# Emitting the rounded copy of a weight piece at the end of the slot that frees its buffer, in the input projections

## The chip, the cores and the metric

The kernel runs on one core of a Trainium2 chip. The metric is the device time of one execution in microseconds (us). A core has five engines that are used here: TensorE (PE; its weight loads are shown apart as PEld), VectorE (DVE), ScalarE (ACT), GpSimd (POOL) and SyncE (SP), whose queue issues most of the DMAs. Each engine takes its instructions strictly in the order in which they were emitted, and waits on semaphores for the others.

## What is computed

One inference step of a two-layer backbone on 128 prompt tokens and 512 latent tokens of width 2048. Layer 0 has attention heads of two kinds (a windowed one with rotary embedding, and a neighbourhood one), layer 1 has bidirectional retention. Cut to the products that matter here:

```python
hp = rmsnorm(xp, norm_pre[l]) * (1.0 + sc_p[:, None]) + sh_p[:, None]
op, ka, va, kb, vb = even_context(hp, w_in_even[i], w_out_even[i], a_sink[i])
os_ = even_latent(hs, w_in_even[i], w_out_even[i], a_sink[i], na_rpb[i], ...)
op, sf, sb = retention_mixer(hp, w_in_odd[i], w_out_odd[i], ...)
xp = xp + g_p[:, None] * rmsnorm(op, norm_post[l])
```

So four large matrix products follow each other: `w_in_even`, `w_out_even`, `w_in_odd`, `w_out_odd`. Attention, retention and the modulation of layer 1 (`adaln`, a product of one vector with `w_ada`) are done beside them.

## The kernel before

**Slots.** The four projections are cut into 732 slots (`slots`, L268 to L278). A slot is one weight piece of 128 x 512 numbers and the matmuls that use it: 24 in a W slot with both token groups (L1370), 30 in an X slot (L1311). Of the 380 W slots of the two input projections, 156 belong to `w_in_even` and 224 to `w_in_odd`. Each product is made of three: the inputs stand in two parts, `hi` and `lo`, and so does each weight piece: `whi` is the piece rounded to fp32r by ScalarE (L291), `wlo` the rest, a subtraction on VectorE that reads `wraw` and `whi` (L292). Both are made in `split_slot`; `whi` and `wlo` have four buffers each, so the parts of slot s + 4 need the buffers that the matmuls of slot s release. The raw piece (`wraw`, five buffers) comes by DMA from SP's queue (`load_slot`, L282).

**What is emitted beside a slot.** At the head of each slot `step_all` takes one step of four lanes: `chain` (norms and residuals between the layers), `rope`, `heads` (attention, later retention) and `adal` (layer 1's modulation). A rope item of layer 0 multiplies on VectorE and GpSimd (L574, L575) and adds on VectorE (L578); one slot later the head's score matmul on TensorE reads the sum `qT` (L722). A block of a head is then a masked sum and maximum on VectorE (L688), an exponential on ScalarE (L698), a normalisation on VectorE (L705), a transpose on TensorE (L742), a copy on ScalarE (L744) and the product with the values (L753). An `adal` step multiplies one or two pieces `adaraw` into two sums `adaacc` on VectorE (L804); in 80 of its units the second product is made by ScalarE (`adaraw` in place, L801) and added by GpSimd (L802).

**Where the split stands.** `ahead(s)` makes the parts of slot s + 4 and issues the load of slot s + 7. `place(s)` says when. It is 2 for the W slots of both input projections: there `ahead(s)` is emitted in the next slot, behind that slot's `step_all`:

```python
step_all()
if s and place(s - 1) == 2:
    ahead(s - 1)
```

It is 1 for X slots and for `w_out_even` (`ahead(s)` at the end of slot s, behind the evacuation of PSUM), and 0 for `w_out_odd` (ahead of the evacuation).

Of the kernel before, what the change touches and what calls it, by code (L numbers as in the profile page):

```python
# [12 lines left out]
F32R = mybir.dt.float32r  # L13
BF16 = mybir.dt.bfloat16
AF = mybir.ActivationFunctionType
# [147 lines left out]
def body(tc, io):  # L163
    nc = tc.nc
# [24 lines left out]
    def dense():  # L189
        return psd.tile([128, 512], F32, name="ps_d", tag="d")  # L190
# [75 lines left out]
    whl = top.enter_context(tc.tile_pool(name="whl", bufs=4))  # L266
# [9 lines left out]
                    continue  # L276
                slots.append((job, kind, role, gs, u0 + u, half, 2 * u + half, 2 * n, w))
    NS = len(slots)  # L278
    raws, halves = {}, {}

    def load_slot(s):
        if s < NS:  # L282
            raws[s] = wraw.tile([128, 512], F32, name="wraw")
            nc.sync.dma_start(raws[s], io["wpack"][slots[s][4]][:, 512 * slots[s][5]:512 * slots[s][5] + 512])

    def split_slot(s):
        if s < NS:
            r = raws.pop(s)
            h = whl.tile([128, 512], F32R, name="whi")
            l = whl.tile([128, 512], F32R, name="wlo")  # L290
            nc.scalar.activation(h, r, AF.Copy)  # L291
            nc.vector.tensor_tensor(l, r, h.bitcast(F32), op=ALU.subtract)  # L292
            halves[s] = (h, l)

    first_ps = []
    with ExitStack() as st:
# [176 lines left out]
        while any(ln.busy() for ln in lanes0):  # L473
            for ln in lanes0:
                ln.step()
            loads(NU)
            if not order and main_loads < RAW:
                load_slot(main_loads)
                main_loads += 1
            while main_splits < main_loads - 1 and ("d", len(FIRST_SEQ) - 4 + main_splits) in done and not w_l.busy():  # L480
                split_slot(main_splits)
                main_splits += 1
# [3 lines left out]
    for i in range(4):  # L486
        if i >= main_splits:
            split_slot(i)
        if i < LEAD:
            load_slot(RAW + i)  # L490
# [11 lines left out]
    def step_all():  # L502
        for ln in lanes:
            ln.step()
# [365 lines left out]
    def norm_state(l):  # L870
        c = ctx.setdefault(("n", l), {})
        return c

    def evac_out(l, n, pss, gs):
        c = norm_state(l)
        cp = c["pool"]
        for gi in gs:
            a, b = GROUPS[gi]
            w = b - a
            ps = pss[gi]  # L880
            if ("acc", gi) not in c:
                c["acc", gi] = cp.tile([128, w], F32, name=f"acc{gi}")
                nc.scalar.activation(c["acc", gi], ps[:, :w], AF.Square)
            else:
                sq = cp.tile([128, 384], F32, name="sq", bufs=2)
                nc.scalar.activation(sq[:, :w], ps[:, :w], AF.Square)  # L886
                if n == KT - 1:
                    c["acc", gi] = [c["acc", gi], sq]
                else:
                    nc.gpsimd.tensor_tensor(c["acc", gi], c["acc", gi], sq[:, :w], op=ALU.add)  # L890
            for a2, b2, v in parts(a, b):
                nc.scalar.activation(y[:, n, a2:b2], ps[:, a2 - a:b2 - a], AF.Copy, scale=gg[l][:, n, v:v + 1])
            if n == 4 and gi == 0:
                for i in range((6, 8)[l]):
                    load_x(l, i)
            if n == KT - 1:
                queue_chain(l, gi)
# [132 lines left out]
    def open_layer1():  # L1030
        st = ExitStack()
        R["st"] = st
        R["qkv"] = st.enter_context(tc.tile_pool(name="qkv", bufs=1))
        R["norm"] = ExitStack()
        norm_state(0)["pool"] = R["norm"].enter_context(tc.tile_pool(name="nrm0", bufs=1))
# [250 lines left out]
    def y_split(k):  # L1286
        nc.scalar.activation(hi[:, k, :], y[:, k, :], AF.Copy)
        nc.vector.tensor_tensor(lo[:, k, :], y[:, k, :], hi[:, k, :].bitcast(F32), op=ALU.subtract)
# [11 lines left out]
    def drain(which):  # L1300
        while any(l.busy() for l in which):
            step_all()

    def X_matmuls(pss, h, l, k0, i, ni, gs):
        for kk in range(2):
            k = k0 + kk
            for p, (xp, wp) in enumerate(((hi, h), (hi, l), (lo, h))):
                for t in range(5):
                    c0 = TP + 128 * t if t < 4 else 0
                    j, o = (t // 2, 256 * (t % 2)) if t < 4 else (2, 0)  # L1310
                    mm(pss[j][:, o:o + 256], lhsT=xp[:, k, c0:c0 + 128], rhs=wp[:, 256 * kk:256 * kk + 256],  # L1311
                       start=(i == 0 and kk == 0 and p == 0 and t in (0, 2, 4)),
                       stop=(i == ni - 1 and kk == 1 and p == 2), skip_group_check=True)

    def ahead(s):

        split_slot(s + 4)
        load_slot(s + LEAD + RAW)

    def place(s):  # L1320

        w, kind = slots[s][8], slots[s][1]
        return PLACE[w, kind]
# [6 lines left out]
    s = 0  # L1330
    while s < NS:
        job, kind, role, gs, unit, half, i, ni, w = slots[s]
        if s == firsts["w_out_even"]:
            drain([rope, heads, adal])
            AB["st"].close()
            L0.close()
            open_layer1()
        if s == firsts["w_in_odd"]:
            pass
        if s == firsts["w_out_odd"]:  # L1340
            drain([heads])
            R["st"].close()
            norm1 = ExitStack()
            chain.new = 1
            norm_state(1)["pool"] = norm1.enter_context(tc.tile_pool(name="nrm1", bufs=1))
        i0 = KP // 4 if role[0] == "rest" else 0
        if i == i0:
            pss = {}
            if kind == "W":
                for gi in gs:  # L1350
                    pss[gi] = dense()
            else:
                for j in range(3):
                    pss[j] = dense()
# [3 lines that stand above are left out]
        if w == "w_in_odd" and i == 0:  # L1358
            chain.new = 2
            for gi in gs:  # L1360
                while ("h1", gi) not in done:
                    step_all()
        h, l = halves.pop(s)
        if kind == "W":
            for kk in range(4):
                k = 4 * i + kk
                for p, (wp, xp) in enumerate(((h, hi), (h, lo), (l, hi))):
                    for gi in gs:
                        a, b = GROUPS[gi]
                        mm(pss[gi][:, :b - a], lhsT=wp[:, 128 * kk:128 * kk + 128], rhs=xp[:, k, a:b],  # L1370
                           start=(k == 4 * i0 and p == 0), stop=(k == KT - 1 and p == 2))
        else:
            X_matmuls(pss, h, l, 2 * i, i, ni, gs)
        if place(s) == 0:
            ahead(s)
        if i == ni - 1:
            if w == "w_in_even":
                evac0(role, pss, gs)
            elif w == "w_in_odd":
                evac1(role, pss, gs)  # L1380
            else:
                evac_out(0 if w == "w_out_even" else 1, role[1], pss, gs)
        if place(s) == 1:
            ahead(s)
        if s in (end0, end1):
            drain([rope, heads] + ([adal] if s == end0 else []))
        for k in ysplit_at.get(s, ()):
            y_split(k)
        s += 1
# [123 lines left out]
```

## Time and profile before

| | |
|---|---|
| Median of 3 runs | 2534.35 us (2533.91 to 2534.43) |
| The profiled execution, its own time | 2534.7 us |
| Its span in the trace | 2532.9 us |
| Busy: PE, PEld, DVE, ACT, POOL | 97%, 94%, 59%, 40%, 15% of the span |
| `w_in_even` slots, by the matmul records of the trace | from 153 us to 989 us |
| `w_in_odd` slots, likewise | from 1231 us to 2278 us |

The span is 1.8 us shorter than the execution's own time, which is 0.35 us above the median. Engine times in the rows are counted from the span's start. A wait is put down to the instruction whose end released it.

### The profile page before, as it was taken

Reading aid. Unit: us, or ns where it says so; the run is one execution under the profiler, and the core shown is the slowest. Engines: PE = TensorE matmul, PEld = TensorE weight load, DVE = VectorE, ACT = ScalarE, POOL = GpSimd, SP = SyncE. Lnnn points to the kernel's source line nnn. Section 1 sums busy time; section 2 is a strip of 40 time slices with the busy share of each in tenths; the row PEclk is TensorE's granted clock in tenths of the full one; section 3 lists DMA queues with packets and bytes.
Section 4 is the critical chain, followed back from the end, with each engine's and each line's share of the span. In section 5 each row is a group of like instructions: output and inputs, shape, how many; then the busy total and the mean of one; then the engine's idle time right before and its main releaser. Section 6 shows DMA issues by size and latency. Waiting matters only on the chain.

```text
span 2532.9 us, 45640 instructions
## 1 busy us (share of the span) xinstructions
PE 2459.2 (97%) x17808; PEld 2383.1 (94%) x17808; DVE 1499.3 (59%) x2834; ACT 1006.8 (40%) x2140; POOL 389.6 (15%) x445
## 2 busy tenths in 40 slices
PE   5999999999999999999999999999999999999997
PEld 3699898999999999998999999999999999999996
DVE  6578787787777875338853535353525355363364
ACT  3233454443343335445653333233323333344443
POOL 1012221112112110114200101010101011011132
PEclk9999999999999999999999999999999999999998
DMA  9855444445545532436543121212121221215374
GB/s 373 319 171 178 148 138 145 127 136 183 174 155 172 174 132 86 160 131 224 188 159 128 63 80 63 88 59 86 61 88 59 80 80 63 80 59 179 124 238 130
DMA packets 186441, 347.12 MB, mean 137 GB/s; under 512 B 20912, under 2 KB 45872, under 8 KB 185712
## 3 DMA queue, kind: packets, MB, share of 16 engines
q1 hardware_dynamic: 182368, 333.25, 39.7%
q0 software_dynamic: 3712, 10.82, 1.2%
q8 instruction: 139, 2.28, 0.4%
q14 instruction: 78, 0.64, 0.1%
q10 hardware_dynamic: 144, 0.13, 0.0%
HBM read 325.51 MB, written 15.99 MB: 135 GB/s over the span
## 4 chain that ended last, share of the span: by engine, by line
PE 69%; DVE 4%; issue 2%; ACT 1%; DMA 1%; POOL 0%; SPq 0%; DVEq 0%; ACTq 0%; POOLq 0%
PE ps_d L1370 49%; PE ps_d L1311 12%; PE ps_O L1250 2%; DVE wlo L292 1%; DVE adaacc L804 1%; PE ps_O L1154 1%; PE ps_S L1154 1%; PE ps_O L753 1%; PE ps_T L1228 1%; ACT whi L291 1%; PE ps_S L1242 1%; DMA wraw<-i_wpack 0%; PE ps_T L742 0%; DVE y L974 0%; PE ps_T L1141 0%
## 5 line engine op out<-in xcount | busy, mean ns | idle before, releaser
L1370 PE MATMUL ps_d<-hi,whi 128*128 128x384 f32 (+1 forms) x3808 | 999.0, 316 | 0.7 <-ACT whi L291 0.6
L1370 PE MATMUL ps_d<-hi,wlo 128*128 128x384 f32 (+1 forms) x3808 | 977.1, 310 | 7.4 <-DVE wlo L292 7.0
L1370 PE MATMUL ps_d<-lo,whi 128*128 128x384 f32 (+1 forms) x3808 | 972.6, 309 | 0.0
L292 DVE TENSOR_TENSOR wlo<-wraw,whi 128x512 fp32r<-128x512 f32 x732 | 565.2, 775 | 595.8 <-ACT whi L291 591.0
L1370 PEld LDWEIGHTS ps_d<-hi,whi 128*128 128x128 f32 x3808 | 632.8, 189 | 11.7 <-issue 4.3
L1370 PEld LDWEIGHTS ps_d<-hi,wlo 128*128 128x128 f32 x3808 | 628.9, 189 | 13.0 <-DVE wlo L292 12.2
L1370 PEld LDWEIGHTS ps_d<-lo,whi 128*128 128x128 f32 x3808 | 628.2, 188 | 0.0
L291 ACT ACTIVATE whi<-wraw 128x512 fp32r<-128x512 f32 x732 | 454.8, 626 | 432.9 <-PE ps_d L1370 220.6
L804 DVE SCALAR_TENSOR_TENSOR adaacc<-adaraw,cvec,adaacc 128x512 f32<-128x512 f32 x400 | 276.8, 743 | 5.8 <-POOL adaacc L802 5.7
L802 POOL TENSOR_TENSOR adaacc<-adaacc,adaraw 128x512 f32<-128x512 f32 x80 | 103.0, 1288 | 714.0 <-ACT adaraw L801 711.2
L1311 PE MATMUL ps_d<-whi,hi 128*128 128x256 f32 x960 | 150.9, 287 | 0.8 <-ACT qT L654 0.8
L1311 PE MATMUL ps_d<-whi,lo 128*128 128x256 f32 x960 | 144.3, 280 | 0.0
L1311 PE MATMUL ps_d<-wlo,hi 128*128 128x256 f32 x960 | 144.3, 280 | 0.0
L801 ACT ACTIVATE adaraw<-adaraw,cvec 128x512 f32<-128x512 f32 x80 | 57.9, 724 | 207.7 <-DVE adaacc L804 149.3
L1311 PEld LDWEIGHTS ps_d<-whi,hi 128*128 128x128 f32 x960 | 128.0, 188 | 4.9 <-issue 1.4
L1311 PEld LDWEIGHTS ps_d<-wlo,hi 128*128 128x128 f32 x960 | 126.5, 188 | 0.0
L1311 PEld LDWEIGHTS ps_d<-whi,lo 128*128 128x128 f32 x960 | 126.5, 188 | 0.0
L890 POOL TENSOR_TENSOR acc<-acc,sq 128x384 f32<-128x384 f32 (+1 forms) x56 | 56.1, 1002 | 425.9 <-ACT sq L886 425.6
L698 ACT ACTIVATE p<-p,small 128x384 f32<-128x384 f32 (+1 forms) x64 | 42.9, 671 | 148.3 <-DVE small L690 148.3
L1146 DVE SCALAR_TENSOR_TENSOR fr<-ps_T,kdec,fr 128x256 fp32r<-128x256 f32 x64 | 31.0, 484 | 95.8 <-ACT fr L1145 95.8
L1235 ACT ACTIVATE sS<-sT 128x128 fp32r<-128x128 f32 x40 | 12.4, 311 | 147.9 <-DVE sT L1234 147.9
L1262 POOL TENSOR_TENSOR mv<-mv,mhalf 128x1 f32<-128x1 f32 x40 | 22.1, 552 | 299.5 <-DVE mv L1261 299.5
(248 smaller groups left out, 2427.8 us busy)
## 6 DMA issues: line engine op xcount, KB each, us to landing
wraw<-i_wpack SPq DMA_DIRECT2D x732, 256.0 KB, 2.8
adaraw<-i_ada SPq DMA_DIRECT2D x256, 256.0 KB, 2.7
sraw<-i_ada SPq DMA_DIRECT2D x64, 512.0 KB, 6.3
y<-i_xTp SPq DMA_DIRECT2D x4, 1280.0 KB, 8.6
wf<-i_wfirst SPq DMA_DIRECT2D x20, 256.0 KB, 5.9
bias<-i_biasB POOLq DMA_DIRECT2D x8, 640.0 KB, 4.9
x_scratch<-y SPq DMA_DIRECT2D x8, 384.0 KB, 3.8
xres<-x_scratch SPq DMA_DIRECT2D x8, 384.0 KB, 6.9
```

The lines of the kernel that those rows point to most:

```text
L291: nc.scalar.activation(h, r, AF.Copy)
L292: nc.vector.tensor_tensor(l, r, h.bitcast(F32), op=ALU.subtract)
L698: nc.scalar.activation(p[:, :nk], src, AF.Exp, bias=sm[:, 0:1], accum_out=sm[:, 1:2])
L801: nc.scalar.activation(r, r, AF.Copy, scale=cvec[:, kt, 1:2])
L802: nc.gpsimd.tensor_tensor(accs[1], accs[1], r, op=ALU.add)
L804: nc.vector.scalar_tensor_tensor(accs[v], r, cvec[:, kt, v:v + 1], accs[v], op0=ALU.mult, op1=ALU.add)
L890: nc.gpsimd.tensor_tensor(c["acc", gi], c["acc", gi], sq[:, :w], op=ALU.add)
L1146: nc.vector.scalar_tensor_tensor(t[:, 1, :], ps[:, :256], R["kdec"][:, d, h:h + 1], t[:, 0, :].bitcast(F32), op0=ALU.mult, op1=ALU.subtract)
L1154: mm(ps[:, 256 * d:256 * d + 256], lhsT=k[:, kp, 128 * d:128 * d + 128], rhs=v[:, vp, ch, :], start=(i == 0), stop=(i == 2))
L1250: mm(ab, lhsT=t["q"][:, qp, d, :], rhs=t["S"][d][sp].rearrange("p i e -> p (i e)"), start=(d == 0 and i == 0), stop=(d == 1 and i == 2))
L1311: mm(pss[j][:, o:o + 256], lhsT=xp[:, k, c0:c0 + 128], rhs=wp[:, 256 * kk:256 * kk + 256], start=(i == 0 and kk == 0 and p == 0 and t in ( ...
L1370: mm(pss[gi][:, :b - a], lhsT=wp[:, 128 * kk:128 * kk + 128], rhs=xp[:, k, a:b], start=(k == 4 * i0 and p == 0), stop=(k == KT - 1 and p = ...
```

## The change

In the W slots of the two input projections the rounded copy `whi` of slot s + 4 is emitted at the end of slot s, behind the evacuation. The subtraction `wlo` and the load stay where they were, behind the next slot's `step_all`. X slots and the output projections keep their order. Nothing is added or left out.

```diff
+    def split_hi(s):
+        if s < NS and s not in his:
+            h = his[s] = whl.tile([128, 512], F32R, name="whi")
+            nc.scalar.activation(h, raws[s], AF.Copy)
+
     def split_slot(s):
         if s < NS:
-            r = raws.pop(s)
-            h = whl.tile([128, 512], F32R, name="whi")
+            split_hi(s)
+            r, h = raws.pop(s), his.pop(s)
             l = whl.tile([128, 512], F32R, name="wlo")
-            nc.scalar.activation(h, r, AF.Copy)
             nc.vector.tensor_tensor(l, r, h.bitcast(F32), op=ALU.subtract)
             halves[s] = (h, l)
...
         if place(s) == 1:
             ahead(s)
+        elif place(s) == 2:
+            split_hi(s + 4)
```

The order of the instructions on VectorE, TensorE, GpSimd and SP is the same in both kernels; ScalarE's is not.

ScalarE in `w_in_even`, around the end of the fourth slot of one job, before (`wraw_2499` is the raw piece whose copy is followed here; `qT` and `rp` are the evacuation of a query head, `adaraw` the in-place product of the modulation):

```order
L291 ACTIVATE whi_2572<-wraw_2446 128x512
L609 ACTIVATE qT_2603<-ps_d_2416 128x128
L563 ACTIVATE rp_2602<-ps_d_2416 128x2x8x16
L564 ACTIVATE rp_2602<-ps_d_2417 128x2x8x16
L801 ACTIVATE adaraw_2565<-adaraw_2565,cvec_75 128x512
L291 ACTIVATE whi_2619<-wraw_2499 128x512
L291 ACTIVATE whi_2659<-wraw_2537 128x512
L801 ACTIVATE adaraw_2653<-adaraw_2653,cvec_75 128x512
L291 ACTIVATE whi_2696<-wraw_2576 128x512
```

The same place in the changed kernel:

```order
L805 ACTIVATE adaraw_2528<-adaraw_2528,cvec_75 128x512
L613 ACTIVATE qT_2603<-ps_d_2418 128x128
L567 ACTIVATE rp_2602<-ps_d_2418 128x2x8x16
L568 ACTIVATE rp_2602<-ps_d_2419 128x2x8x16
L289 ACTIVATE whi_2608<-wraw_2499 128x512
L805 ACTIVATE adaraw_2567<-adaraw_2567,cvec_75 128x512
L289 ACTIVATE whi_2649<-wraw_2537 128x512
L289 ACTIVATE whi_2689<-wraw_2576 128x512
L805 ACTIVATE adaraw_2655<-adaraw_2655,cvec_75 128x512
```

The copies of `wraw_2499` and `wraw_2576` stand ahead of the `adaraw` product that stood ahead of them.

ScalarE in `w_in_odd`, where a slot's steps transpose a retention key (`fr` is its rounded, decayed copy), before:

```order
L1072 ACTIVATE k1_15804<-ps_d_15638 128x256
L1145 ACTIVATE fr_15812<-ps_T_15809,kdec_15652 128x256
L291 ACTIVATE whi_15815<-wraw_15708 128x512
L1145 ACTIVATE fr_15866<-ps_T_15863,kdec_15652 128x256
L1145 ACTIVATE fr_15869<-ps_T_15863,kdec_15652 128x256
L291 ACTIVATE whi_15872<-wraw_15747 128x512
```

And in the changed kernel:

```order
L1076 ACTIVATE k1_15804<-ps_d_15638 128x256
L289 ACTIVATE whi_15807<-wraw_15708 128x512
L1149 ACTIVATE fr_15814<-ps_T_15811,kdec_15652 128x256
L289 ACTIVATE whi_15845<-wraw_15747 128x512
L1149 ACTIVATE fr_15868<-ps_T_15865,kdec_15652 128x256
L1149 ACTIVATE fr_15871<-ps_T_15865,kdec_15652 128x256
```

Each copy of a piece now stands ahead of the key copies of the next slot's head step.

## Rows read from the trace of the kernel before

**Rows 1.** Page: each engine's busy us (share of the span) xinstructions.

```profile
PE 2459.2 (97%) x17808; PEld 2383.1 (94%) x17808; DVE 1499.3 (59%) x2834; ACT 1006.8 (40%) x2140; POOL 389.6 (15%) x445
```

**Rows 2.** Busy us (xinstructions) of PE, PEld, DVE, ACT, POOL; clock; DMA share; GB/s.

```profile
153.00:515.00 362.00, 347.99 (x2485) 338.43 (x2484) 291.37 (x553) 158.64 (x346) 83.02 (x89) 0.99 0.48 152
515.00:975.00 460.00, 455.87 (x3484) 442.74 (x3483) 345.51 (x682) 180.52 (x386) 78.90 (x85) 1.00 0.48 156
...
1400.00:2200.00 800.00, 800.00 (x5842) 792.49 (x5841) 361.62 (x714) 261.01 (x581) 95.33 (x140) 1.00 0.22 73
```

**Rows 3.** TensorE's waits from 153 to 515 us: total us, times, longest.

```profile
PE ps_S L722 <- DVE qT L578: 10.3, 4, 4.3
PE ps_T L742 <- DVE p L705: 1.8, 3, 0.7
PE ps_S L725 <- DVE small L688: 1.6, 1, 1.6
```

**Rows 4.** TensorE's waits from 515 to 975 us.

```profile
PE ps_T L742 <- DVE p L705: 2.0, 2, 1.7
PE ps_d L1311 <- ACT qT L654: 0.8, 1, 0.8
```

**Rows 5.** TensorE's waits from 1186 to 2270 us, the only row.

```profile
PE ps_d L1370 <- DVE wlo L292: 1.2, 3, 0.6
```

**Rows 6.** Waits of VectorE and of ScalarE from 153 to 515 us.

```profile
DVE wlo L292 <- ACT whi L291: 61.1, 45, 4.2
...
ACT adaraw L801 <- DVE adaacc L804: 66.9, 24, 5.0
ACT p L698 <- DVE small L690: 62.5, 27, 6.9
```

**Rows 7.** Timeline around TensorE's longest wait (start us, us, engine line op [idle before <-releaser]).

```profile
411.84 0.72 ACT L801 ACTIVATE adaraw<-adaraw,cvec 128x512 f32<-128x512 f32 x1 [3.63 <-DVE adaacc L804]
412.47 0.62 ACT L291 ACTIVATE whi<-wraw 128x512 fp32r<-128x512 f32 x1
412.65 1.29 POOL L802 TENSOR_TENSOR adaacc<-adaacc,adaraw 128x512 f32<-128x512 f32 x1 [3.97 <-ACT adaraw L801]
...
413.12 1.37 DVE L292 TENSOR_TENSOR wlo<-wraw,whi 128x512 fp32r<-128x512 f32 x1 [1.31 <-ACT whi L291]
...
417.38 0.46 PE L1370 MATMUL ps_d<-hi,wlo 128*128 128x384 f32 x2
...
420.12 1.34 DVE L292 TENSOR_TENSOR wlo<-wraw,whi 128x512 fp32r<-128x512 f32 x1 [1.36 <-ACT whi L291]
...
421.38 0.68 DVE L578 TENSOR_TENSOR qT<-qT,rp 128x512 f32<-128x512 f32 x1
...
422.12 0.79 PE L722 MATMUL ps_S<-kT,qT 128*128 128x256 f32 x1 [4.28 <-DVE qT L578]
```

**Rows 8.** All `wlo` subtractions (ns min/median/max), and the modulation's sums (busy us, mean ns).

```profile
L292 DVE TENSOR_TENSOR wlo<-wraw,whi x732: 675/693/2331, 144.3 to 2507.2; 128x512 fp32r<-128x512 f32 x183
L804 DVE SCALAR_TENSOR_TENSOR adaacc<-adaraw,cvec,adaacc 128x512 f32<-128x512 f32 x400 | 276.8, 743 | 5.8 <-POOL adaacc L802 5.7
L802 POOL TENSOR_TENSOR adaacc<-adaacc,adaraw 128x512 f32<-128x512 f32 x80 | 103.0, 1288 | 714.0 <-ACT adaraw L801 711.2
```

**Rows 9.** Two short stretches behind the two longest waits; the clock is the column behind POOL's.

```profile
270.10:273.40 3.30, 3.30 (x14) 3.30 (x13) 2.89 (x7) 0.34 (x1) 0.00 (x0) 0.50 0.49 171
422.10:427.00 4.90, 4.88 (x17) 4.70 (x18) 4.76 (x10) 2.89 (x7) 0.00 (x0) 0.50 0.64 206
```

**Rows 10.** The window from 153 to 515 us, GpSimd's sums L802 alone.

```profile
153.00:515.00 362.00, 46.43 (x36) 0.99 0.48 152
```

**Rows 11.** Timeline of one retention key in `w_in_odd`.

```profile
1754.99 0.62 ACT L291 ACTIVATE whi<-wraw 128x512 fp32r<-128x512 f32 x1
...
1755.13 0.48 DVE L1146 SCALAR_TENSOR_TENSOR fr<-ps_T,kdec,fr 128x256 fp32r<-128x256 f32 x1 [0.37 <-ACT fr L1145]
...
1757.87 0.87 PE L1154 MATMUL ps_O<-v,fr 128*128 128x256 f32 x6
```

More of the change, by code (lines that the diff above doesn't have):

```diff
@@ L278, in body @@
     NS = len(slots)
-    raws, halves = {}, {}
+    raws, his, halves = {}, {}, {}
     def load_slot(s):
```

## The prediction

> **What bounds the kernel now.** I read the page first, then the busy time by stretch, then TensorE's waits in each stretch, and last the timeline around its longest waits. TensorE is busy for 2459.2 of 2532.9 us [rows 1]. From 1400 to 2200 us, most of `w_in_odd`, it is busy for all of 800.00 us [rows 2]: there nothing that another engine does sooner can help, and something later can only harm. What the change can win lies in `w_in_even`: 362 - 347.99 = 14.0 us of idle TensorE from 153 to 515 us, and 460 - 455.87 = 4.1 us from 515 to 975 us [rows 2]. The waits say on whom: up to 515 us nearly all are on VectorE, 10.3 us on the rotary sum `qT`, 1.8 us on the normalised `p` and 1.6 us on the maximum `small`, 13.7 us together [rows 3].
>
> VectorE is not full there. It is busy for 291.37 of 362 us [rows 2], and 61.1 us of the rest are 45 waits of `wlo` for `whi` [rows 6]. ScalarE is emptier still, 158.64 us busy [rows 2], but waits for VectorE: 66.9 us ahead of `adaraw` and 62.5 us ahead of the exponential `p` [rows 6]. So the two wait for each other in a ring. The timeline shows one turn of it: VectorE finishes a sum, ScalarE makes `adaraw` (411.84, 0.72 us), only then `whi` (412.47, 0.62 us), and VectorE, whose next instruction is `wlo`, has stood still for 1.31 us. A second turn costs 1.36 us before 420.12. Meanwhile TensorE ends its slot at 417.38 + 0.46 = 417.84 us and waits until 422.12 for the sum L578, which VectorE reaches at 421.38 [rows 7].
>
> No wait of ScalarE on TensorE stands in front of `whi` among the large waits of this stretch [rows 6]: the buffer that `whi` needs has long been free, and the copy is late only because of what is queued ahead of it.
>
> **The change, part by part.** (1) In 156 W slots of `w_in_even`, `whi` moves in front of the next slot's `adaraw` and exponential. It then waits for nothing that VectorE makes in that step, and `wlo` finds it ready. Each turn gives VectorE some 1.3 us back [rows 7].
>
> (2) `wlo` itself gets shorter. In the turns it takes 1.37 and 1.34 us [rows 7], against a median of 0.693 us [rows 8]: it starts while GpSimd's sum L802 runs (412.65, 1.29 us) and ends about one normal `wlo` after it [rows 7]. When `wlo` no longer waits, it runs while ScalarE still makes `adaraw`, before GpSimd starts. That is 0.67 us more in each of the 36 such units before 515 us [rows 10].
>
> (3) Sum at the longest wait: the rotary sum would start 1.31 + 1.36 + 2 x 0.67 = 4.0 us sooner, at 417.4 instead of 421.38, and end at 418.1 us, 0.2 us after TensorE's slot. That removes all but 0.2 us of 4.28 us, with what VectorE wins in earlier slots not yet counted [rows 7]. For the whole stretch: without the waits for `whi` VectorE needs some 300 of the 348 us that TensorE is busy, so it can catch up everywhere but in short bursts. I take 13 of the 13.7 us [rows 3] as gone.
>
> (4) The clock. After the two longest waits the granted clock is 0.50, that is 1.2 GHz instead of 2.4, for 3.30 and 4.90 us [rows 9]; TensorE had stood idle just before both. At half speed half of this is lost, 8.2 / 2 = 4.1 us. With the waits gone I expect no drop: 4 us.
>
> (5) From 515 to 975 us TensorE's waits are 3.9 us in all, the largest 2.0 us on `p` and 0.8 us on an evacuation [rows 4]. X slots stand here too, and their split does not move; I take half, 2 us.
>
> (6) In `w_in_odd` the only wait is 1.2 us on `wlo` at its start [rows 5], where VectorE works on the norm between the layers; 1 us.
>
> (7) What is added is a wait: `whi` now stands on ScalarE's queue until TensorE has ended slot s, with the next slot's copies behind it. In layer 0 those mostly read what TensorE writes after slot s, or what VectorE makes later, so the wait replaces one that is there anyway, and the copy itself costs them 0.62 us [rows 7] once a slot. In `w_in_odd` the tightest thing behind it is a retention key: its low part ends at 1755.13 + 0.48 = 1755.61 and TensorE reads it at 1757.87, so 2.26 us are spare against 0.62 us [rows 11]. `adaraw` goes later against the copy, with GpSimd's sum and the reload of its tile on SP's queue; with four tiles and at most two units a slot, the next unit that needs that tile is two slots away or more. The loads of `wraw` follow `wlo` on SP's queue and can only come sooner. Bounds for (7): 0 us, and for the worst see the slow rival. I take 2.5 us, for short waits that take the place of the old ones.
>
> Sum: 13 + 4 + 2 + 1 - 2.5 = 17.5 us. From the profiled execution's 2534.7 us that is 2517.2; the median stands 0.35 us lower, so I say **2517 us**. If every idle stretch named went and nothing came in its place, the gain would be 13.7 + 4.1 + 3.9 + 1.2 = 22.9 us, 2511 us.
>
> **A rule that speaks against (2).** The rows show `wlo` at twice its length while GpSimd adds two SBUF tiles [rows 7, 8]. The Trainium skill has a rule for it (SBUF — State Buffer, section "Who interferes with whom"): a VectorE instruction with two SBUF inputs and a GpSimd instruction that reads SBUF exclude each other, and the second to start waits for the first to end. The rows of `wlo` agree; by this rule the sums L804, which also read two SBUF tiles, would clash in its place, which no row here shows, since none of them runs beside L802 before. What that does to the time is the second case below.
>
> **The rivals.** *GpSimd takes ScalarE's place.* After `wlo` VectorE goes straight into the next step's sums. Suppose the first of them (0.743 us, [rows 8]) holds GpSimd up, as GpSimd now holds `wlo` up [rows 7]; the second needs the tile that GpSimd writes. From the end of the sum that `adaraw` follows: `wlo` 0.69 and a sum 0.74 make 1.4 us (`adaraw`, 0.72, is done by then); GpSimd's 1.29 make it 2.7 us; then comes the second sum. Before, the same sum started after 1.31 + 1.37 + 0.74 = 3.4 us. The gain of a turn falls from 2.0 to 0.7 us. Over 36 units that is 25 us instead of 72, still more than the lateness at the longest wait but not enough in every burst. I let a third of (3), of (5) and of the clock stay: 6 us less, **2523 us**. For it: the units follow each other closely. Against it: heads' instructions often lie between. The exclusion in the Trainium skill's page SBUF — State Buffer, cited above, would bring this about.
>
> *VectorE is late by its own work.* Between 153 and 515 us it is 80% busy [rows 2]; where several steps meet in a slot of 3.5 us no wait for `whi` need be involved, and the same sums reach TensorE as late as before, or ScalarE's `whi` sits behind an evacuation that is itself late. Then the change does not do what it is about: no more than the 2 to 4 us of some turns, within 3 us of **2532 us**. Against it: at the longest wait the turns alone make up 4.0 of 4.28 us [rows 7].
>
> *ScalarE is held by TensorE.* In `w_in_odd` each W slot's `whi` now holds ScalarE until the slot ends, and the key copies behind it reach TensorE late. It decides from the point where a key is pushed by more than the 2.26 us that are spare [rows 11]. If every one of the 64 keys in W slots (224 of 288) lost one copy, 64 x 0.62 x 224 / 288 = 31 us would come on top of the gain: 2517 + 31 = **2548 us**. Against it: 0.62 us is a quarter of what is spare, and ScalarE is a third busy there [rows 2].
>
> **How the numbers follow.** Forecast 0.66, GpSimd 0.18, VectorE's own work 0.11, ScalarE held 0.05. A measurement of this kernel can tell 0.2%, 5 us, from no change. The first two cases gain over 5 us nearly always, 0.83; the third lies within it, 0.12 with the tail of the second; slower 0.05. The range takes the full gain as its low end, 2511, and covers the GpSimd case up to 2530, beyond which lie the last two cases.
>
> **What would show it.** In the profile after: the waits of `wlo` for `whi` between 153 and 515 us fall from 61 us to under 15; VectorE's busy time there falls by about 20 us, from shorter `wlo`; TensorE's waits on `qT` fall from 10.3 us to under 2; no stretch at clock 0.50 between 270 and 430 us; new waits of ScalarE's `whi` on TensorE in layer 0; from 1400 to 2200 us still no wait of TensorE. The forecast is wrong if TensorE still waits 5 us or more on `qT`, or if VectorE's waits on L802, 5.7 us in the whole kernel [rows 8], rise to tens of us and TensorE's stay.

## The result, and the profile after

| | before | after |
|---|---|---|
| Median (lowest to highest), 4 runs each | 2534.39 us (2533.91 to 2534.63) | 2509.17 us (2508.59 to 2510.49) |
| The profiled execution, and its span | 2534.7, 2532.9 us | 2509.1, 2507.3 us |

The ratio is 0.99 (95% interval 0.9888 to 0.9912): 25.2 us, 1.0%, faster. The direction is as forecast. The gain was put at 17.5 us, and the time lies 1.8 us below the low end of the range, 2511 us.

Line numbers after are 2 to 4 away from those before: `whi` is L289, `wlo` L296, the modulation's product `adaraw` L805, GpSimd's sum L806, VectorE's sum L808, the rotary sum `qT` L582, its score matmul L726, the exponential L702, a W slot's matmul L1374. The page's line of busy time, to be set against [rows 1]:

```profile
PE 2451.5 (98%) x17808; PEld 2379.4 (95%) x17808; DVE 1485.8 (59%) x2834; ACT 1024.3 (41%) x2140; POOL 397.4 (16%) x445
```

The same stretches as in [rows 2] (PE, PEld, DVE, ACT, POOL, clock, DMA share, GB/s):

```profile
153.00:515.00 362.00, 362.00 (x2660) 355.30 (x2659) 303.91 (x585) 174.96 (x373) 93.03 (x97) 1.00 0.52 162
515.00:975.00 460.00, 459.47 (x3470) 447.70 (x3469) 337.96 (x677) 193.73 (x398) 73.60 (x77) 1.00 0.47 153
...
1400.00:2200.00 800.00, 800.00 (x5843) 792.49 (x5841) 361.83 (x714) 266.78 (x580) 96.84 (x140) 1.00 0.22 73
```

From 153 to 515 us TensorE is now busy without a gap, and the clock is 1.00 throughout. 2660 matmuls fit where 2485 did. The work of the old stretch now ends at about 496 us, so the next rows go to 496 us. TensorE's waits from 153 to 965 us are a single one, where [rows 3, 4] show five rows:

```profile
PE ps_d L832 <- DVE adab L818: 0.4, 1, 0.4
```

VectorE's two waits that matter here, from 153 to 496 us (total us, times, longest):

```profile
DVE adaacc L808 <- POOL adaacc L806: 12.1, 10, 1.4
...
DVE wlo L296 <- ACT whi L289: 6.4, 4, 4.2
```

And the three largest of ScalarE in the same stretch:

```profile
ACT whi L289 <- PE ps_d L1374: 37.9, 29, 2.9
ACT adaraw L805 <- DVE adaacc L808: 37.2, 25, 2.9
ACT p L702 <- DVE small L694: 29.8, 20, 2.5
```

Against [rows 6], VectorE's wait for `whi` went from 61.1 to 6.4 us. ScalarE waits for VectorE less (66.9 to 37.2 and 62.5 to 29.8 us). In exchange its copy waits for TensorE to release the buffer, 37.9 us, a wait that was not among the large ones before; TensorE, with one wait of 0.4 us, shows no harm from it in these slots.

The place of the longest wait, now 15 us earlier, shows the new order (start us, us, engine, line, operation; to be set beside [rows 7]):

```profile
398.80 0.63 ACT L289 ACTIVATE whi<-wraw 128x512 fp32r<-128x512 f32 x1 [0.46 <-PE ps_d L1374]
...
400.37 2.67 DVE L808 SCALAR_TENSOR_TENSOR adaacc<-adaraw,cvec,adaacc 128x512 f32<-128x512 f32 x3
...
402.96 0.68 DVE L296 TENSOR_TENSOR wlo<-wraw,whi 128x512 fp32r<-128x512 f32 x1
403.12 0.72 ACT L805 ACTIVATE adaraw<-adaraw,cvec 128x512 f32<-128x512 f32 x1 [2.92 <-DVE adaacc L808]
403.56 0.68 DVE L582 TENSOR_TENSOR qT<-qT,rp 128x512 f32<-128x512 f32 x1
403.92 1.47 POOL L806 TENSOR_TENSOR adaacc<-adaacc,adaraw 128x512 f32<-128x512 f32 x1 [2.76 <-ACT adaraw L805]
404.36 2.24 DVE L808 SCALAR_TENSOR_TENSOR adaacc<-adaraw,cvec,adaacc 128x512 f32<-128x512 f32 x2
...
406.64 0.46 PE L1374 MATMUL ps_d<-hi,wlo 128*128 128x384 f32 x2
...
406.94 0.59 PE L726 MATMUL ps_S<-kT,qT 128*128 128x256 f32 x2
```

`whi` ends at 399.43 us, 3.5 us before VectorE comes to `wlo`, and waited for TensorE alone. `wlo` starts as soon as the sums are done, beside `adaraw`, takes 0.68 us where it took 1.37, and `qT` ends at 404.24, 2.7 us before TensorE wants it. Before, it ended at 422.06 us, 4.2 us after TensorE's slot.

**Where the 25.6 us between the two spans lie.** The two traces hold the same 17808 matmuls in the same order, so the distance from one start to the next can be compared one by one. Added up: 20.89 us in the slots from 153 to 516 us (before's time), 4.84 from 516 to 989 us, 0.94 behind that, and a loss of 1.11 us ahead of 153 us, together 25.6. Of the 20.89 us, 15.31 lie at the nine waits of over 0.15 us, 3.87 in matmuls at half clock, and 1.71 at small matmuls behind a wait or under a shown gap of 0.12 us.

### The profile page after: what moved, and what is told of

Its sections match the earlier page's. It is cut to its first block, busy times and chain, and to the rows that moved or that the text cites. A ratio compares the mean times of both kernels' runs of the same rounds, so it can differ in the third digit from the quotient of the medians.

```text
span 2507.3 us, 45634 instructions
## 1 busy us (share of the span) xinstructions
PE 2451.5 (98%) x17808; PEld 2379.4 (95%) x17808; DVE 1485.8 (59%) x2834; ACT 1024.3 (41%) x2140; POOL 397.4 (16%) x445
## 3 DMA queue, kind: packets, MB, share of 16 engines
q1 hardware_dynamic: 182368, 333.25, 40.3%
## 4 chain that ended last, share of the span: by engine, by line
PE 94%; DVE 3%; DMA 1%; ACT 1%; issue 1%; POOL 0%; SPq 0%; DVEq 0%; ACTq 0%; POOLq 0%
PE ps_d L1374 64%; PE ps_d L1315 14%; PE ps_d L433 3%; PE ps_O L757 2%; PE ps_O L1254 2%; PE ps_T L746 1%; PE ps_S L1158 1%; PE ps_O L1158 1%; PE ps_S L729 1%; PE ps_T L1232 1%; DVE wlo L296 1%; PE ps_S L346 1%; PE ps_S L732 1%; PE ps_T L346 1%; PE ps_S L1246 1%
## 5 line engine op out<-in xcount | busy, mean ns | idle before, releaser
L1374 PE MATMUL ps_d<-hi,whi 128*128 128x384 f32 (+1 forms) x3808 | 997.3, 316 | 0.1
L1374 PE MATMUL ps_d<-hi,wlo 128*128 128x384 f32 (+1 forms) x3808 | 975.9, 310 | 8.3 <-DVE wlo L296 8.0
L1374 PE MATMUL ps_d<-lo,whi 128*128 128x384 f32 (+1 forms) x3808 | 971.5, 309 | 0.0
L296 DVE TENSOR_TENSOR wlo<-wraw,whi 128x512 fp32r<-128x512 f32 x732 | 524.1, 719 | 480.9 <-ACT whi L289 477.7
L289 ACT ACTIVATE whi<-wraw 128x512 fp32r<-128x512 f32 x732 | 459.4, 630 | 753.3 <-PE ps_d L1374 450.1
L1374 PEld LDWEIGHTS ps_d<-hi,whi 128*128 128x128 f32 x3808 | 631.7, 189 | 10.9 <-issue 4.3
L1374 PEld LDWEIGHTS ps_d<-hi,wlo 128*128 128x128 f32 x3808 | 627.9, 188 | 13.7 <-DVE wlo L296 12.8
L1374 PEld LDWEIGHTS ps_d<-lo,whi 128*128 128x128 f32 x3808 | 627.2, 188 | 0.0
L808 DVE SCALAR_TENSOR_TENSOR adaacc<-adaraw,cvec,adaacc 128x512 f32<-128x512 f32 x400 | 295.2, 786 | 23.8 <-POOL adaacc L806 23.4
L806 POOL TENSOR_TENSOR adaacc<-adaacc,adaraw 128x512 f32<-128x512 f32 x80 | 108.8, 1361 | 680.9 <-ACT adaraw L805 680.9
L805 ACT ACTIVATE adaraw<-adaraw,cvec 128x512 f32<-128x512 f32 x80 | 58.0, 724 | 139.0 <-DVE adaacc L808 97.8
L702 ACT ACTIVATE p<-p,small 128x384 f32<-128x384 f32 (+1 forms) x64 | 43.0, 672 | 84.9 <-DVE small L694 84.8
L1218 POOL TENSOR_TENSOR qS<-q,qS 128x256 fp32r<-128x256 f32 x32 | 23.6, 737 | 300.1 <-ACT qS L1217 300.1
```

What stands on the lines that cost most here:

```text
L289: nc.scalar.activation(h, raws[s], AF.Copy)
L805: nc.scalar.activation(r, r, AF.Copy, scale=cvec[:, kt, 1:2])
L806: nc.gpsimd.tensor_tensor(accs[1], accs[1], r, op=ALU.add)
L808: nc.vector.scalar_tensor_tensor(accs[v], r, cvec[:, kt, v:v + 1], accs[v], op0=ALU.mult, op1=ALU.add)
```

## The experiments

The theory: the ring of [rows 7] cost the time, VectorE waiting for `whi`, `whi` queued behind `adaraw`, `adaraw` waiting for VectorE's sum. The rivals: VectorE being late by its own work, GpSimd's exclusion, and an effect of `w_in_odd`. Runs 1 to 4 share 17 runs of the kernel before (median 2534.95 us), 5 and 6 share 7 (2535.51), 7 and 8 share 7 (2534.75). The edits of runs 4 and 5 are shown against the kernel before, those of the others against the changed kernel; `...` stands for code left out.

**1 and 2: one layer at a time.** The changed kernel with its last lines limited:

```diff
-        elif place(s) == 2:
+        elif place(s) == 2 and w == "w_in_even":
```

> The early copy in the 156 W slots of w_in_even alone. Theory (all that was won lies in layer 0, where VectorE no longer waits for a copy queued behind ScalarE's steps): the whole gain stays, and the 1.5 us wait of TensorE on wlo that came up at the start of w_out_odd goes again, 2507.7 us, 2507 to 2509. Rival (the 224 slots of w_in_odd have a part in the gain, by the 1 us at its start or by loads that come sooner): 2510.5 us or more.

Measured: 2508.11 us (2507.91 to 2509.23), ratio 0.9896 (0.9883 to 0.991). The other half has `w == "w_in_odd"` in that line:

> The early copy in the 224 W slots of w_in_odd alone. Theory: TensorE has no wait there to lose, 2534.4 us less 0.1 at its start plus 1.5 at the start of w_out_odd, 2535.8 us, 2534 to 2537. Rival (it has a part in the gain): under 2532 us.

Measured: 2535.9 us (2534.72 to 2537.87), ratio 1.0005 (0.9996 to 1.0014). Its VectorE waits in layer 0 are those of before, and in `w_in_odd` TensorE is as full as before; the first row is of the waits from 153 to 515 us, the second of the busy time by stretch:

```profile
DVE wlo L296 <- ACT whi L289: 61.1, 45, 4.2
```
```profile
1400.00:2200.00 800.00, 800.00 (x5841) 792.49 (x5841) 361.74 (x714) 267.01 (x580) 96.93 (x140) 1.00 0.23 73
```

The whole gain is `w_in_even`'s. The 224 copies moved in `w_in_odd` are worth nothing that can be measured. The rival in which they hold ScalarE did not occur at the retention keys; in a small form it did behind them, at the change to `w_out_odd`: there this run's trace has the wait of TensorE of 1.6 us that is shown below for the changed kernel.

**3: the copy in front of `adaraw` only.** In `w_in_even` it is emitted between the next slot's heads step and its `adal` step: still behind the exponential, but ahead of `adaraw`. The end of a slot emits nothing.

```diff
-        step_all()
+        for ln in lanes:
+            if ln is adal and s and place(s - 1) == 2 and slots[s - 1][8] == "w_in_even":
+                split_hi(s + 3)
+            ln.step()
...
         elif place(s) == 2:
-            split_hi(s + 4)
+            pass
```

> In w_in_even the copy is emitted behind the head step but still ahead of the modulation's step: ScalarE's exponential stands ahead of it, adaraw behind it. Theory (the turn through adaraw, 1.3 us and a longer wlo each, is what made VectorE late): most of the gain stays, 2509 to 2514 us, and VectorE's waits of wlo for whi up to 515 us are under 25 us. Rival (the turn through the exponential has as large a part): 2518 us or more, waits over 35 us.

Measured: 2508.4 us (2507.41 to 2508.82), ratio 0.9896 (0.9882 to 0.9909), the whole gain and 0.6 us below what was expected. VectorE's wait for the copy from 153 to 515 us:

```profile
DVE wlo L296 <- ACT whi L289: 14.9, 12, 4.2
```

Having the copy behind the exponential leaves 12 waits, but TensorE waits for 0.3 us in all from 153 to 965 us. So it is the turn through `adaraw` that cost the time.

**4: everything at the end of the slot.** Copy, subtraction and load together, as X slots have it. On ScalarE the copy then stands where the change puts it.

```diff
-PLACE = {("w_in_even", "W"): 2, ("w_in_even", "X"): 1, ("w_out_even", "W"): 1, ("w_in_odd", "W"): 2,
+PLACE = {("w_in_even", "W"): 1, ("w_in_even", "X"): 1, ("w_out_even", "W"): 1, ("w_in_odd", "W"): 2,
```

> The kernel before with the whole split of w_in_even's W slots, copy, subtraction and load, at the end of the slot. Theory (VectorE has some 45 us to spare in 362, so that waiting for TensorE's slot end ahead of the next step's sums costs it little): 2509 to 2514 us. Rival (a subtraction that holds VectorE until the slot ends makes its sums late, and TensorE waits for the heads again): 2518 us or more, with waits on qT or p of 5 us and more.

Measured: 2543.31 us (2541.19 to 2543.95, 6 runs), ratio 1.0033 (1.0021 to 1.0045): slower than before; the expected gain did not come, and the rival's waits on `qT` did. The ring is there in full. Waits of VectorE from 153 to 520 us, of TensorE from 153 to 515 us, and the timeline of one turn:

```profile
DVE wlo L292 <- ACT whi L291: 76.6, 50, 4.2
```
```profile
PE ps_S L722 <- DVE qT L578: 12.8, 5, 5.8
```
```profile
415.57 2.07 DVE L804 SCALAR_TENSOR_TENSOR adaacc<-adaraw,cvec,adaacc 128x512 f32<-128x512 f32 x3
...
417.68 0.72 ACT L801 ACTIVATE adaraw<-adaraw,cvec 128x512 f32<-128x512 f32 x1 [3.62 <-DVE adaacc L804]
...
418.30 0.62 ACT L291 ACTIVATE whi<-wraw 128x512 fp32r<-128x512 f32 x1
...
418.95 1.37 DVE L292 TENSOR_TENSOR wlo<-wraw,whi 128x512 fp32r<-128x512 f32 x1 [1.31 <-ACT whi L291]
```

This is the turn of [rows 7]: the same 1.31 us of waiting and the same `wlo` of 1.37 us. The copy is as early as in the change, but the subtraction moved with it: it follows the very sum that the `adaraw` ahead of the copy waits for. What counts is not how early ScalarE makes the copy, but that VectorE has something else to do between that sum and `wlo`. (It is 8.4 us slower than before, and not equal. Matched start by start, its trace loses 8.2 us in the slots from 153 to 516 us, 6.3 of them at fourteen waits of TensorE that are new or longer; those on `qT` add up to 2.5 us more. Why VectorE is later there than before was not tried.)

**5 and 6: the ring opened at its other end.** All 80 products that ScalarE makes as `adaraw` go to VectorE; `whi` stays where it was before (5), or where the change puts it (6). VectorE gets more work, GpSimd's L802 goes.

```diff
-                ada_items.append([[lambda i=i0 + j, p=(j == 1 and i0 % KT < 12): ada_unit(i, p) for j in range(n)],
+                ada_items.append([[lambda i=i0 + j, p=False: ada_unit(i, p) for j in range(n)],
```

> The order of the kernel before, but all second products of the modulation on VectorE: no adaraw on ScalarE, no sum on GpSimd, 80 more sums of 0.743 us on VectorE. Theory (each unit through ScalarE and GpSimd costs VectorE 1.3 us of waiting and 0.67 us of a longer wlo, more than the 0.743 us that it saves): faster than the kernel before, 2512 to 2524 us. Rival (VectorE is late by its own work): slower, 2540 us or more.

Measured (5): 2507.35 us (2505.92 to 2508.29), ratio 0.9891 (0.9875 to 0.9908). Busy time and VectorE's wait for `whi` from 153 to 500 us:

```profile
153.00:500.00 347.00, 347.00 (x2533) 340.30 (x2532) 296.64 (x603) 142.17 (x321) 37.79 (x56) 1.00 0.54 163
```
```profile
DVE wlo L292 <- ACT whi L291: 26.9, 19, 5.0
```

It beat what was expected of it. VectorE does 296.64 us of work in 347 us (291.52 in the changed kernel's same window), and TensorE has no wait at all from 153 to 965 us. So VectorE's own load was not what made `qT` late before, and the 19 waits for the copy that are left cost nothing.

> The changed order, and all second products of the modulation on VectorE. Theory: once the copy is early, a unit through ScalarE and GpSimd does save VectorE up to 0.743 us; VectorE gets 36 x 0.743 = 27 us more work up to 515 us, of which it has some 45 to spare, so TensorE waits again only in bursts: 2510 to 2516 us. Rival (VectorE stays ahead of TensorE anyway, and loses GpSimd's interference): 2509 us or less.

Measured (6): 2509.96 us (2507.22 to 2510.35), ratio 0.9898 (0.9883 to 0.9913), between the two cases. Both openings together give no more than one; this run cannot be told from the change by itself.

**7: late copy, later subtraction.** The copy stays where it was before, behind the next slot's steps. `wlo` and the load come one slot's steps later.

```diff
         step_all()
+        flush()
         if s and place(s - 1) == 2:
-            ahead(s - 1)
+            if slots[s - 1][8] == "w_in_even":
+                split_hi(s + 3)
+                pending.append(s - 1)
+            else:
+                ahead(s - 1)
```

(`flush` emits the pending `split_slot` and `load_slot`; `ahead` calls it first, and the end of a slot emits no copy.)

> In w_in_even's W slots the copy stays where it was before the change, behind the next slot's steps, and the subtraction and the load go one slot later, behind the steps of the slot after. Theory (what counts is that a whole step of VectorE's work stands between ScalarE's copy and VectorE's subtraction, not that the copy is early): TensorE's waits on qT, p and small go, 2507 to 2513 us, and VectorE's waits of wlo for whi up to 515 us are under 20 us. Rival (the copy must be early, because adaraw and the exponential hold it back): 2528 to 2540 us.

Measured: 2510.08 us (2509.71 to 2511.8), ratio 0.9904 (0.9887 to 0.992). VectorE's wait from 153 to 515 us, and TensorE's waits from 153 to 965 us:

```profile
DVE wlo L296 <- ACT whi L289: 6.2, 3, 4.2
```
```profile
PE ps_S L726 <- DVE qT L582: 0.6, 1, 0.6
PE ps_d L832 <- DVE adab L818: 0.4, 1, 0.4
```

The copy is as late as before, and nearly the whole gain is there. With run 4, this settles it: what is needed is distance between the copy and its reader, whichever of the two moves. A whole step is enough here, and in run 3 the modulation's step alone. In the slots from 153 to 516 us the traces of runs 1, 3, 5 and 7 win 20.9 us each, as the changed kernel does.

**8: the same for `w_out_even`.** As run 1, and in addition `("w_out_even", "W"): 2`, with the early copy there too.

> The early copy in w_in_even and, with the subtraction behind the next slot's steps, also in w_out_even; w_in_odd as before the change. TensorE's 3.7 us of waits on wlo from 1100 to 1160 us are the question. Theory (VectorE is busy 30.55 of the 32 us in which they lie, so it is bound by its own work there): no more than 1 us against the early copy in w_in_even alone, 2507 to 2509 us. Rival (the same turn between the two engines makes them): 2503 to 2506 us.

Measured: 2508.56 us (2508.31 to 2510.27), ratio 0.99 (0.9885 to 0.9914): no gain over run 1. Busy time in a stretch of `w_out_even`, and TensorE's wait from 975 to 1186 us:

```profile
1120.00:1152.00 32.00, 27.82 (x210) 25.64 (x209) 32.00 (x42) 17.84 (x39) 17.94 (x15) 1.00 0.76 245
```
```profile
PE ps_d L1374 <- DVE wlo L296: 4.4, 10, 1.6
```

In run 1 the same window has VectorE busy for 30.54 us, and TensorE waits for 3.7 us. With the distance VectorE is full, 32.00 of 32 us, and TensorE waits no less: the cure is for an engine that waits, not for one that works.

The best that was run are 5, 1 and 3, at 2507.35, 2508.11 and 2508.4 us. Their ranges overlap, and none is clearly apart from the others.

## Why the prediction was right in its mechanism and too small

**The ring, (1) and (3): right, mis-sized.** The wait for `whi`, 61 us before, was to fall under 15, and is 6.4; the waits on `qT` were to fall under 2, and are gone; ScalarE's new waits on TensorE came. Runs 3, 4, 5 and 7 show that the ring through `adaraw` is the cause. But 13 us was taken from idle time as the profile shows it [rows 3], and that undercounts here. In a full stretch a matmul starts 0.16 us before the modelled end of the one before: L726 starts at 406.94, and the matmuls ahead of it end at 406.64 + 0.46 = 407.10. At the nine longest waits of this stretch one shown as g costs 0.14 to 0.16 us more than g. At the longest the start came 4.56 us behind the last one and now comes 0.12 behind it: 4.44 us lost where 4.28 are shown. These nine waits, all of over 0.15 us from 153 to 516 us, add up to 13.9 us shown and cost 15.31; 1.71 us more lay in small matmuls behind a wait. So this term was 17.0 us, not 13.

**The clock, (4): right.** 3.87 us against 4. No half clock is left between 270 and 430 us.

**515 to 975 us, (5): the step that chose half.** The reason given, that X slots' splits do not move, did not hold: the stretch lost all its idle but 0.5 us, and 4.84 us came back where 2 were taken, more even than the 3.9 us of the waits. Four of these waits, shown as 3.5 us together, stood in X slots, at 532, 540, 639 and 731 us, and all four went, although X slots keep their order. That VectorE came to them sooner because it had lost less in the W slots ahead is likely, but no run takes this stretch by itself.

**The start of `w_in_odd`, (6): too large.** 0.1 us instead of 1. Some 0.85 us came ahead of it, on a wait at 1185 us that the prediction did not list. That the two together come near 1 us is luck: in the traces of the other runs this place gives from 0.9 us more to 0.8 us less than before.

**The deduction, (7): it did not come in layer 0.** 2.5 us were taken off for waits that take the place of the old ones. In layer 0 a single wait of 0.4 us is left, and that one stood there before as well. The one new wait is elsewhere, in the fourth slot of `w_out_odd`, whose weight piece is copied at the end of `w_in_odd`. There ScalarE also casts the next projection's input (`hi`), and VectorE subtracts it (`lo`). Before, ScalarE went from the copy into the casts without a wait:

```profile
2264.91 0.62 ACT L291 ACTIVATE whi<-wraw 128x512 fp32r<-128x512 f32 x1
2265.44 2.61 ACT L1287 ACTIVATE hi<-y 128x640 fp32r<-128x640 f32 x4
```

After, at the same place and behind it (rows of several timelines):

```profile
2241.36 0.63 ACT L289 ACTIVATE whi<-wraw 128x512 fp32r<-128x512 f32 x1 [1.79 <-PE ps_d L1374]
2241.90 2.61 ACT L1291 ACTIVATE hi<-y 128x640 fp32r<-128x640 f32 x4
...
2242.65 3.03 DVE L1292 TENSOR_TENSOR lo<-y,hi 128x640 fp32r<-128x640 f32 x4 [0.88 <-ACT hi L1291]
...
2255.76 0.62 ACT L289 ACTIVATE whi<-wraw 128x512 fp32r<-128x512 f32 x1
...
2256.28 2.61 ACT L1291 ACTIVATE hi<-y 128x640 fp32r<-128x640 f32 x4
...
2259.99 2.49 DVE L296 TENSOR_TENSOR wlo<-wraw,whi 128x512 fp32r<-128x512 f32 x4
2260.73 0.44 PE L1374 MATMUL ps_d<-hi,wlo 128*128 128x384 f32 x1 [1.62 <-DVE wlo L296]
```

The copy holds ScalarE for 1.79 us until TensorE has freed its buffer, and the casts wait behind it. Against TensorE's matmuls VectorE is then 0.9 us later than before. Another copy, at 2255.76, that has come to stand ahead of the last casts makes it 1.5 us, and TensorE stands for 1.62 us. So ScalarE held by TensorE did cost something, 1.48 us by the distances between starts, and the prediction had looked for it at the wrong place: it named a retention key as the tightest thing behind the copy, and it was these casts. With `w_in_odd` left as it was (run 1) that wait is absent. Behind 2440 us some 1.6 us came back, so in this trace the two cancel; but run 1 has 1.0 and run 5 1.4 us there too, so that is not this order's doing.

**The range.** Its low end was reasoned as "If every idle stretch named went and nothing came in its place, the gain would be 13.7 + 4.1 + 3.9 + 1.2 = 22.9 us". That was taken for a ceiling, but it was a sum of idle times as shown, without what each wait costs beside them. This is the step that put the time outside the range: the waits of the first stretch, priced at 13.7 us in this sum, cost 17.0 us, and those of the second, priced at 3.9, cost 4.84. By the measured terms: 17.0 + 3.87 + 4.84 + 0.94 - 1.1 = 25.6 us, with the loss of 1.1 us ahead of 153 us, which nothing in the prediction stands for.

**The shorter `wlo`, (2), and GpSimd.** The time of all `wlo` and of all VectorE's modulation sums in the slots from 153 to 515 us, first before:

```profile
153.00:515.00 362.00, 77.87 (x79) 0.99 0.48 152
...
153.00:515.00 362.00, 125.23 (x181) 0.99 0.48 152
```

and in the same slots after:

```profile
153.00:496.00 343.00, 55.87 (x80) 1.00 0.52 162
...
153.00:496.00 343.00, 137.64 (x181) 1.00 0.52 162
```

`wlo` gave back 22.0 us, where 36 x 0.67 = 24 were forecast. The sums took 12.4 of them again: 32 of the 400 now run beside GpSimd's sum, where none did before, as at 404.36 us, where two take 2.24 us instead of 1.49. GpSimd's sum grew too, and VectorE waits for it for 23.4 us instead of 5.7 [rows 8] (groups of the whole kernel: busy us, mean ns, idle before):

```profile
L808 DVE SCALAR_TENSOR_TENSOR adaacc<-adaraw,cvec,adaacc 128x512 f32<-128x512 f32 x400 | 295.2, 786 | 23.8 <-POOL adaacc L806 23.4 <-DMA adaraw<-i_ada 0.2
```
```profile
L806 POOL TENSOR_TENSOR adaacc<-adaacc,adaraw 128x512 f32<-128x512 f32 x80 | 108.8, 1361 | 680.9 <-ACT adaraw L805 680.9
```

The normalisation `p` (L705, after L709) took 11.4 us more: 13 of its 33 instructions there now stand beside GpSimd's sum and take 1.3 to 1.6 us instead of 0.3 to 0.5. First its time before, then after, then one such pair from the timeline after:

```profile
153.00:515.00 362.00, 15.20 (x32) 0.99 0.48 152
...
153.00:496.00 343.00, 26.64 (x33) 1.00 0.52 162
...
342.33 1.27 POOL L806 TENSOR_TENSOR adaacc<-adaacc,adaraw 128x512 f32<-128x512 f32 x1 [7.96 <-ACT adaraw L805]
342.35 1.54 DVE L709 TENSOR_SCALAR p<-p,small 128x512 f32<-128x512 f32 x1
```

The rotary product (L574, after L578) gave 5.7 us back. So the second case's mechanism came, without its price: VectorE's busy time in the same slots did not fall by the 20 us forecast, only from 291.37 [rows 2] to 287.56 us (22.0 + 5.7 - 12.4 - 11.4 = 3.9), yet TensorE lost nothing. What the change removed is VectorE's waiting, not its work. The next row is of all its work there:

```profile
153.00:496.00 343.00, 343.00 (x2499) 336.35 (x2498) 287.56 (x557) 167.87 (x357) 86.43 (x90) 1.00 0.52 162
```

The prediction named this as a sign that it was wrong only if TensorE's waits stayed, and they went. The Trainium skill's rule (SBUF — State Buffer, section "Who interferes with whom"), that a VectorE instruction with two SBUF inputs and a GpSimd instruction that reads SBUF exclude each other, agrees with the rows of the subtraction and the sums. The clash passed on from the subtraction to the sums and to the normalisation.

**VectorE late by its own work, and ScalarE held:** the first did not occur, by run 5. The second did not occur at the keys, by run 2; at the casts behind them it cost the 1.48 us above.

## What to carry to other kernels

When two in-order engines hand work to each other in both directions within one step, look for the ring: a consumer emitted straight behind its own engine's part of the step waits for a producer that is queued behind that part's result. Put some of the consumer engine's other work between the two, up to one step; either may move, and moving both together won nothing here (run 4). Look at what stands behind the producer in its queue: here a copy that waits for TensorE held up casts. And price a wait of the bound engine by the distance between starts: at the nine long waits here the idle that the profile shows was less than what they cost.

## What was not expected

- **A wait costs more than the idle shown**, by some 0.16 us each, and the next small matmul comes late as well: at 305.85 us before, 0.32 us behind the last start, where the changed kernel has 0.22.
- **Half clock behind idle.** Before, the granted clock was 0.50 for 3.41 us after an idle of 3.66 us, and for 6.83 us (from 420.26 us) around the one of 4.28 us; the waits of 1.6 us had none. In run 4 both last 6.8 us (PE busy first). That does not come from its order: in run 2, where layer 0 has the order of before, the first also lasts 6.83 us, around the same idle of 3.66 us.

```profile
269.90:276.70 6.80, 5.19 (x19) 5.02 (x20) 5.49 (x11) 1.24 (x4) 0.00 (x0) 0.50 0.68 211
427.00:433.80 6.80, 4.36 (x15) 4.19 (x16) 5.68 (x12) 3.75 (x8) 0.00 (x0) 0.50 0.47 155
```

- **A dip whose cause is open.** After, the clock is also 0.50 at 40.3 to 43.6 us, ahead of all slots, where the instructions are the same in both kernels. TensorE had waited for 2.14 and 1.98 us shortly before, and in the kernel before for 2.02 and 1.99 us with no dip. By the distances between starts it costs 1.5 us; 0.4 us came back ahead of it. The profiles of runs 1, 3, 6, 7 and 8 have it too, at about the same time; those of before and of runs 2, 4 and 5 have not. So part of run 5's small lead may be this and not its order. What brings it on was not tried and stays open. The row is of the changed kernel:

```profile
40.30:43.60 3.30, 3.30 (x23) 1.76 (x22) 3.20 (x8) 1.53 (x3) 0.00 (x0) 0.50 1.02 403
```
